# Causal attention on one NeuronCore: the high and low halves of the values held side by side as one 128-column weight

## The chip, the cores and the metric

The kernel runs on one core of a Trainium2 chip. The metric is the device time of one execution in microseconds (us); lower is better. Products run on TensorE (PE, with its weight loads shown apart as PEld), element-wise work on VectorE (DVE), ScalarE (ACT) and GpSimd (POOL). Products write to PSUM, an accumulator memory of eight banks with 512 float32 columns each; everything else lies in SBUF.

## The reference

A decoder trunk of two layers over 1024 positions with 1024 features. The first layer mixes latent attention (8 heads, keys of 96, values of 64) and a short gated convolution, the second is a state-space mixer, and each is followed by a gated feed-forward part with a short convolution. Only the attention matters here:

```python
def causal_block_attention(q, k, v):
    for i in range(seq // Q_BLOCK):          # 8 blocks of 128 queries
        lo, hi = i * Q_BLOCK, (i + 1) * Q_BLOCK
        s = jnp.einsum("bqhd,bkhd->bhqk", q[:, lo:hi], k[:, :hi]).astype(jnp.float32) * scale
        s = jnp.where(causal, s, -jnp.inf)
        p = jax.nn.softmax(s, axis=-1).astype(v.dtype)
        outs.append(jnp.einsum("bhqk,bkhd->bqhd", p, v[:, :hi]))
```

Everything is float32. The kernel keeps that precision by splitting an operand into a high part, rounded to the type float32r, and a low part, the rest. A product of two such operands is made from three: high by high, high by low, low by high (`PASSES` in the code).

## The kernel before

Attention is one stage of the kernel, between the input projection and the first feed-forward part. Its order is written out by hand; the instructions of an engine run in the order of the code. Eight steps (`Step`) cover four groups (`gr`) of two heads and two halves (`hf`) of the 1024 positions. A step has eight items (`Item`): four blocks of 128 queries (`i`) by two heads (`h`). The block number is `qb` = 4 hf + i, and the item takes in `qb` + 1 blocks of 128 keys. Over all items that makes 8 heads x 36 = 288 blocks of keys.

For one item, in turn:

- `scores` (TensorE): three products per 512 keys into a PSUM tile `pss`, weights `qh` or `ql` of 128 columns, moving `kh` or `kl`; then the mask as a product of `tri` and `eye`.
- `exponent`: VectorE takes the maximum of a row (`nm`), ScalarE the exponential (`pr`) and its sum. `invert` and `normalize` (VectorE) divide by that sum.
- `turn` (TensorE): the probabilities are transposed, 128 by 128, into `ptp`. ScalarE copies out the high part (`ph`, or `pair` for the second head), VectorE the low part (`lows`).
- `values` (TensorE, line 634): per block of keys three products into `po`, with the values as weight, 64 columns each: `vh` with the high probabilities, `vh` with the low, `vl` with the high.

The loop over items is pipelined: while the scores of item j are made, item j - 2 is transposed and item j - 3 meets its values. Between them stand parts of later steps: query and key products, their norms, their transposes (ScalarE makes `qh` and `kh`, VectorE `ql` and `kl`), and rows of the output projection (`row_down`), which VectorE adds to `xT`.

A PSUM tile `po` of one bank takes four items: two heads, 256 columns apart, by two blocks of queries. After the fourth, `finish_pair` copies it into the tile `a32` on ScalarE, one copy per head, rounds that to `ath` on ScalarE, and GpSimd subtracts to get `atl`. There are sixteen such finished pairs. In the order on VectorE, `finish_pair` lies behind the low parts and the sums of the item (`lows`, `others`) and ahead of the reciprocal (`invert`) and the next row addition and maximum:

```python
it.exponent()
...
others.get(j, nothing)()
finish = retire(queue.pop(0)) if len(queue) > 3 else nothing
finish()
it.invert()
```

Of the kernel before, what the change touches and what calls it, by code (L numbers as in the profile page):

```python
# [14 lines left out]
AF = mybir.ActivationFunctionType  # L15
ALU = mybir.AluOpType
# [4 lines left out]
P = 128  # L21
# [9 lines left out]
VD = 64  # L31
# [19 lines left out]
def hybrid_trunk_kernel(ctx: ExitStack, tc: tile.TileContext, xt, gains, mix_w_in, w_uq, w_ukv, q_gain, k_gain,  # L51
                        mix_w_out, ssm_w_in, lambda_re, lambda_im, log_step, b_re, b_im, c_re, c_im, d_skip, w_glu,
                        ffn_w_up, ffn_w_down, rope_cos, rope_sin, causal, eye16, halves, out, dbg=None):
    nc = tc.nc
# [112 lines left out]
    PASSES = ((0, 0), (0, 1), (1, 0))  # L167
# [103 lines left out]
    for gr in range(2):  # L271
        gts = []
        for i in range(2):
# [6 lines left out]
            t = pB.tile([P, S + 2], F32, tag="ut", name="ut")  # L280
# [27 lines left out]
    with phase("pc") as pC, tc.tile_pool(name="psa", bufs=1, space=PSUM, reuse_waits="tile") as pa:  # L308
# [38 lines left out]
        for tabs, row in ((tabq, qrow), (tabk, krow)):  # L347
            for j, (tab, g0) in enumerate(((cos_t, NOPE), (sin_t, NOPE + 16), (cos_t, NOPE + 16), (sin_t, NOPE))):
                nc.gpsimd.tensor_tensor(out=tabs[j], in0=tab,
                                        in1=row[:, g0:g0 + 16].unsqueeze(1).broadcast_to([P, NB, 16]),  # L350
                                        op=ALU.mult)
# [79 lines left out]
        class Step:  # L431
# [20 lines left out]
            def kv_products(self, c, bank=ps_p):  # L452
                gr, hf = self.gr, self.hf
                if c == 0:
                    self.kn = qtile("kn")
                    vt = (atile if gr % 2 else lambda name: vtile(name, F32R))("vt")
                    vv = vt.rearrange("p (t i h n) -> p t i h n", t=2, i=4, h=2)
                    self.vh, self.vl = vv[:, 0], vv[:, 1]
                ps = bank("pkv")
                for i in range(2):  # L460
                    b = 4 * hf + 2 * c + i
                    for k in range(2):
                        for ci, wi in PASSES:
                            nc.tensor.matmul(ps[:, 256 * i:256 * i + 256], lhsT=ckT[k][ci][:, P * b:P * b + P],
                                             rhs=wkv[k][wi][:, 256 * gr:256 * gr + 256],
                                             start=(k == 0 and ci == 0 and wi == 0), stop=(k == 1 and ci == 1))
                pf = ps.rearrange("p (a n) -> p a n", n=P)
                kf = self.kn.rearrange("p i h n -> p (i h) n")
                vhf = self.vh.rearrange("p i h n -> p (i h) n")[:, 4 * c:4 * c + 4, :]
                vlf = self.vl.rearrange("p i h n -> p (i h) n")[:, 4 * c:4 * c + 4, :]  # L470
                nc.scalar.activation(vhf, pf[:, :, NOPE:P], AF.Copy)
                nc.scalar.activation(kf[:, 4 * c:4 * c + 4, 0:NOPE], pf[:, :, 0:NOPE], AF.Copy)
                nc.vector.tensor_tensor(out=vlf, in0=pf[:, :, NOPE:P], in1=vhf.bitcast(F32), op=ALU.subtract)
# [77 lines left out]
        both = lambda f, *args: [f(c, *args) for c in range(2)]  # L551
# [6 lines left out]
        for n in range(8):  # L558
            if n == 4:
                wkv = [split_w(w, nc.vector) for w in wkv_raw]  # L560
            kind, p = ("kv", "q")[n // 4], n % 4
# [10 lines left out]
        class Item:  # L572
# [57 lines left out]
            def values(self, po, c0):  # L630
                for kb in range(self.qb + 1):
                    sk = self.steps[kb // 4]
                    for vi, pi in PASSES:
                        nc.tensor.matmul(po[0:VD, c0:c0 + P], lhsT=(sk.vh, sk.vl)[vi][:, kb % 4, self.h, :],  # L634
                                         rhs=self.pt[kb // 4][pi][:, P * (kb % 4):P * (kb % 4) + P],
                                         start=(kb == 0 and vi == 0 and pi == 0), stop=(kb == self.qb and vi == 1))

        def row_down(k, f):

# [12 lines left out]
        def finish_pair(grp, po, hf, i2):  # L652
            a32 = small([P, 256], "a32", "a32", 1)
            for h in range(2):
                nc.scalar.activation(a32[VD * h:VD * h + VD, :], po[0:VD, 256 * h:256 * h + 256], AF.Copy)
            cols = slice(HALF * hf + 256 * i2, HALF * hf + 256 * i2 + 256)
            nc.scalar.activation(grp.at[0][:, cols], a32, AF.Copy)
            nc.gpsimd.tensor_tensor(out=grp.at[1][:, cols], in0=a32, in1=grp.at[0][:, cols].bitcast(F32),
                                    op=ALU.subtract)
# [5 lines left out]
        def retire(item):  # L665
            st, i, h = item.st, item.i, item.h
            if i % 2 == 0 and h == 0:
                st.po = ps_t("po")
            item.values(st.po, 256 * h + P * (i % 2))
            if i % 2 == 0 or h == 0:  # L670
                return lambda: None

            def finish():
                if st.hf == 0 and i == 1:
                    groups[st.gr] = Group(st.gr)
                finish_pair(groups[st.gr], st.po, st.hf, i // 2)
                if st.hf == 1 and i == 3 and st.gr < 2:
                    rows_left.extend((st.gr, f) for f in range(KT))

            return finish  # L680
# [1084 lines left out]
    for m in range(FIRST, NM):  # L1765
        p = pairs[m]
# [106 lines left out]
```

## Time and profile before

| | |
|---|---|
| Time, median of 3 runs (lowest to highest) | 2345.22 us (2342.04 to 2348.31) |
| The profiled execution's own time | 2344.66 us |
| Its span, first to last instruction | 2342.9 us |
| Instructions | 29810 |
| PE busy over the span | 2248.5 us, 96% |
| DVE busy | 1614.7 us, 69% |
| ACT busy | 851.3 us, 36% |
| POOL busy | 767.0 us, 33% |
| Stretch of the scores and values | about 275 to 512 us |

The profile is one execution of the program, taken by the hardware. A busy share is an average over stages with different limits, and TensorE's products are pipelined: a product's record of 220 ns overlaps those before and behind it, so what counts is the distance from one to the next. The time of a change is read from the stage in which it lies and from the chain of work that ended last there.

### The profile page before, as it was taken

The page shows a single profiled execution, that of the slowest core. Times are in us where ns is not written, and L with a number is a line of the kernel's source. Part 1 is how long each engine was busy: PE and PEld are TensorE (multiplying, and loading weights), DVE is VectorE, ACT ScalarE, POOL GpSimd, SP SyncE. Part 2 cuts the span into 40 slices and gives each one's busy share as a digit, 9 for nine tenths or more (in the row PEclk, how much of TensorE's full clock was granted, in tenths as well). Part 3 has the DMA queues.
Part 4 walks back from the last instruction along what each step waited for, and adds up shares of the span by engine and source line. Part 5 has one row for each costly group of instructions (what it writes and reads, how often), then busy time and mean ns, then how long its engine had stood idle before and what let it go on. Part 6 is the DMA issues. An engine that isn't in the chain of part 4 may idle for free.

```text
span 2342.9 us, 29810 instructions
## 1 busy us (share of the span) xinstructions
PE 2248.5 (96%) x11228; PEld 1867.9 (80%) x11228; DVE 1614.7 (69%) x2650; ACT 851.3 (36%) x1446; POOL 767.0 (33%) x575
## 2 busy tenths in 40 slices
PE   7999899999999999999999988999789999999999
PEld 6888888888788878888888877788568888878887
DVE  6344677787978778879777487323888888876542
ACT  4112566664232333332223255312444444443110
POOL 4322454435233222232224344431043333324220
PEclk9999999999999999999999998999999999999999
DMA  4112000012122221223332288521132222245301
GB/s 155 45 38 57 1 10 10 10 46 72 29 66 62 82 68 49 76 80 92 101 102 63 93 223 242 171 72 41 54 110 93 82 81 81 81 153 181 125 10 72
DMA packets 227152, 192.04 MB, mean 82 GB/s; under 512 B 25472, under 2 KB 202944, under 8 KB 227008
## 3 DMA queue, kind: packets, MB, share of 16 engines
q1 hardware_dynamic: 227008, 190.14, 26.9%
q8 instruction: 88, 1.44, 0.2%
q14 instruction: 56, 0.46, 0.1%
HBM read 148.22 MB, written 46.07 MB: 83 GB/s over the span
## 4 chain that ended last, share of the span: by engine, by line
PE 79%; DVE 11%; issue 3%; DMA 3%; ACT 3%; POOL 1%; SPq 0%; DVEq 0%; POOLq 0%; ACTq 0%
PE pu L175 31%; PE pd L190 22%; PE pc L1648 4%; PE pb L1648 4%; PE pa L1648 4%; PE pd L1648 2%; PE pu L1554 1%; PE pss L586 1%; PE po L634 1%; PE pckv L378 1%; PE pq L446 1%; PE ptp L615 1%; DVE xT L1696 1%; PE pcq L378 1%; PE pda L644 1%
## 5 line engine op out<-in xcount | busy, mean ns | idle before, releaser
L154 POOL TENSOR_TENSOR wl<-raw,wh 128x1024 fp32r<-128x1024 f32 (+2 forms) x115 | 289.1, 2515 | 487.3 <-ACT wh L153 242.3
L193 DVE TENSOR_TENSOR xT<-pd,xT 128x512 f32<-128x512 f32 x320 | 204.3, 682 | 160.4 <-PE pd L190 159.8
L153 ACT ACTIVATE wh<-raw 128x1024 fp32r<-128x1024 f32 (+2 forms) x117 | 122.4, 1051 | 305.8 <-PE pu L175 212.6
L175 PE MATMUL pu<-f_h,wh 128*128 128x512 f32 x704 | 219.4, 393 | 0.0
L175 PE MATMUL pu<-f_l,wh 128*128 128x512 f32 x704 | 217.2, 390 | 0.0
L175 PE MATMUL pu<-f_h,wl 128*128 128x512 f32 x704 | 216.7, 389 | 0.0
L175 PEld LDWEIGHTS pu<-f_l,wh 128*128 128x128 f32 x704 | 132.1, 188 | 27.9
L175 PEld LDWEIGHTS pu<-f_h,wl 128*128 128x128 f32 x704 | 132.1, 188 | 27.9
L175 PEld LDWEIGHTS pu<-f_h,wh 128*128 128x128 f32 x704 | 130.7, 188 | 28.7 <-issue 1.7
L810 POOL TENSOR_TENSOR gl<-c,gh 128x512 fp32r<-128x512 f32 x44 | 61.4, 1415 | 247.0 <-ACT gh L809 247.0
L1696 DVE SCALAR_TENSOR_TENSOR xT<-u,vec,xT 128x1024 f32<-128x1024 f32 x84 | 111.1, 1330 | 13.3 <-ACT xT L1694 12.6
L759 DVE TENSOR_TENSOR u<-pu,f_rb 128x512 f32<-128x512 f32 x88 | 56.8, 685 | 89.9 <-PE pu L175 87.9
L190 PE MATMUL pd<-gh,wh 128*128 128x512 f32 x352 | 113.5, 403 | 5.4 <-DVE u L759 2.9
L190 PE MATMUL pd<-gh,dwh 128*128 128x512 f32 x352 | 108.8, 390 | 2.5 <-DVE xT L193 1.5
L190 PE MATMUL pd<-gl,wh 128*128 128x512 f32 x352 | 110.4, 395 | 0.0
L190 PE MATMUL pd<-gh,wl 128*128 128x512 f32 x352 | 110.0, 394 | 0.0
L190 PE MATMUL pd<-gh,dwl 128*128 128x512 f32 x352 | 108.5, 389 | 0.0
L190 PE MATMUL pd<-gl,dwh 128*128 128x512 f32 x352 | 108.4, 389 | 0.0
L1796 POOL TENSOR_TENSOR dwl<-raw,dwh 128x1024 fp32r<-128x1024 f32 x20 | 60.8, 3066 | 112.5 <-PE pd L190 84.3
L761 ACT ACTIVATE c<-u,vec 128x512 f32<-128x512 f32 x88 | 59.9, 717 | 69.5 <-DVE u L759 69.1
L190 PEld LDWEIGHTS pd<-gh,wh 128*128 128x128 f32 x352 | 65.8, 191 | 22.6 <-DVE xT L193 4.0
L190 PEld LDWEIGHTS pd<-gh,dwh 128*128 128x128 f32 x352 | 66.1, 188 | 16.9 <-DVE xT L193 1.9
(569 smaller groups left out, 5790.6 us busy)
## 6 DMA issues: line engine op xcount, KB each, us to landing
raw<-in_ffn_w_up_dram SPq DMA_DIRECT2D x50, 512.0 KB, 3.8
raw<-in_ffn_w_down_dram SPq DMA_DIRECT2D x42, 512.0 KB, 4.4
xT<-in_ffn_w_up_dram SPq DMA_DIRECT2D x40, 512.0 KB, 3.6
gfd<-xT SPq DMA_DIRECT2D x21, 512.0 KB, 2.6
raw<-gfd SPq DMA_DIRECT2D x20, 512.0 KB, 4.0
raw<-in_w_glu_dram SPq DMA_DIRECT2D x16, 512.0 KB, 4.0
raw<-in_mix_w_in_dram SPq DMA_DIRECT2D x14, 512.0 KB, 3.9
xT<-in_xt_dram SPq DMA_DIRECT2D x8, 512.0 KB, 7.6
```

The lines of the kernel that those rows point to most:

```text
L153: nc.scalar.activation(h[:, 0:n], raw[:, 0:n], AF.Copy)
L154: eng.tensor_tensor(out=l[:, 0:n], in0=raw[:, 0:n], in1=h[:, 0:n].bitcast(F32), op=ALU.subtract)
L175: nc.tensor.matmul(ps[hf], lhsT=w[wi][:, P * k:P * k + P], rhs=xs[k][xi][:, HALVES[hf]], start=(k == 0 and wi == 0 and xi == 0), stop=(k = ...
L190: nc.tensor.matmul(ps[hf], lhsT=ws[i][wi][:, P * f:P * f + P], rhs=gts[i][xi][:, HALVES[hf]], start=(i == first and wi == 0 and xi == 0), ...
L193: nc.vector.tensor_tensor(out=xT[f][:, HALVES[hf]], in0=ps[hf], in1=xT[f][:, HALVES[hf]], op=ALU.add)
L378: nc.tensor.matmul(ps[:, HALF * j:HALF * j + n], lhsT=xa[k][xi][:, P * (2 * p + j):P * (2 * p + j) + P], rhs=w[k // kw][wi][:, n * (k % kw ...
L759: nc.vector.tensor_tensor(out=u[:, 2:HALF + 2], in0=ps[hf], in1=rb[:, HALVES[hf]], op=ALU.mult)
L761: nc.scalar.activation(c, u[:, 2:HALF + 2], AF.Copy, scale=cwcol(layer, 2, m))
L810: nc.gpsimd.tensor_tensor(out=gl[:, cols], in0=cv[hf], in1=gh[:, cols].bitcast(F32), op=ALU.subtract)
L1648: nc.tensor.matmul(ps, lhsT=w[:, HALF * wi + P * k:HALF * wi + P * k + P], rhs=x.at(xi, k), start=(start and k == 0 and wi == 0 and xi == ...
L1696: nc.vector.scalar_tensor_tensor(out=c, in0=u[:, w:S + w], scalar=cwcol(self.layer, w, m), in1=c, op0=ALU.mult, op1=ALU.add)
L1796: eng.tensor_tensor(out=l, in0=raw, in1=h.bitcast(F32), op=ALU.subtract)
```

## The change

The tile of the values, 1024 columns, is laid out anew. Before, all high parts stood ahead of all low parts. Now the high and the low part of one block and head stand side by side, 64 + 64 columns, so that they make one weight of 128 columns. Each block of keys then has two products: this weight with the high probabilities, and with the low ones. The upper 64 rows of the result hold what the high values give, the lower 64 rows what the low values give (the product of low by low comes with it). The two halves are added in `finish_pair`: ScalarE copies the lower half from PSUM, VectorE adds the upper half to it.

```diff
@@ kv_products
-                    vv = vt.rearrange("p (t i h n) -> p t i h n", t=2, i=4, h=2)
-                    self.vh, self.vl = vv[:, 0], vv[:, 1]
+                    vv = vt.rearrange("p (i h t n) -> p i h t n", t=2, i=4, h=2)
+                    self.vh, self.vl = vv[:, :, :, 0], vv[:, :, :, 1]
+                    self.v = vt.rearrange("p (i h n) -> p i h n", i=4, h=2)
@@ values
-                    for vi, pi in PASSES:
-                        nc.tensor.matmul(po[0:VD, c0:c0 + P], lhsT=(sk.vh, sk.vl)[vi][:, kb % 4, self.h, :],
+
+                    for pi in range(2):
+                        nc.tensor.matmul(po[:, c0:c0 + P], lhsT=sk.v[:, kb % 4, self.h, :],
                                          rhs=self.pt[kb // 4][pi][:, P * (kb % 4):P * (kb % 4) + P],
-                                         start=(kb == 0 and vi == 0 and pi == 0), stop=(kb == self.qb and vi == 1))
+                                         start=(kb == 0 and pi == 0), stop=(kb == self.qb and pi == 1))
@@ finish_pair
             for h in range(2):
-                nc.scalar.activation(a32[VD * h:VD * h + VD, :], po[0:VD, 256 * h:256 * h + 256], AF.Copy)
+                rows, both = slice(VD * h, VD * h + VD), slice(256 * h, 256 * h + 256)
+                nc.scalar.activation(a32[rows, :], po[VD:P, both], AF.Copy)
+                nc.vector.tensor_tensor(out=a32[rows, :], in0=po[0:VD, both], in1=a32[rows, :], op=ALU.add)
```

The order of instructions differs at two places that matter. The first is on TensorE, in the last item of the second group's second half (`qb` = 7, eight blocks of keys). A shape there is rows of the result by moving columns. Before:

```order
L532 MATMUL ptqk<-ident,kn 96x128 [waits Pool_49]
L532 MATMUL ptqk<-ident,kn 96x128 x3
L634 MATMUL po<-pair,vt 64x128 x24
L586 MATMUL pss<-kh,qh 128x256 [waits PE_49,Activation_49]
L586 MATMUL pss<-kl,qh 128x256
L586 MATMUL pss<-kh,ql 128x256
```

and with the change:

```order
L533 MATMUL ptqk<-ident,kn 96x128 [waits Pool_49]
L533 MATMUL ptqk<-ident,kn 96x128 x3
L636 MATMUL po<-pair,vt 128x128 x16
L587 MATMUL pss<-kh,qh 128x256 [waits PE_49,Activation_49]
L587 MATMUL pss<-kl,qh 128x256
L587 MATMUL pss<-kh,ql 128x256
```

Twenty-four products have become sixteen, with 128 result rows each in place of 64; what stands around them is the same.

The second is the finished pair of that half's first two blocks, on VectorE. In brackets stand the engines whose semaphore an instruction waits for. Before, VectorE has no part in it:

```order
L627 TENSOR_TENSOR pl<-ptp,ph 128x512 [waits Activation_49]
L627 TENSOR_TENSOR pl<-ptp,ph 128x384 [waits Activation_49]
L535 SCALAR_TENSOR_TENSOR ql<-ptqk,gq,qh 96x512 [waits Activation_49]
L505 TENSOR_REDUCE kv<-sqk 128x4 [waits Activation_49]
L603 RECIPROCAL rs<-sm 128x1
L646 TENSOR_TENSOR xT_90<-pda,xT_90 128x1024
L595 TENSOR_REDUCE nm<-pss 128x1 [waits PE_49]
```

With the change, two additions (`a<-po,a`) stand between the sums `kv` and the reciprocal `rs`:

```order
L628 TENSOR_TENSOR pl<-ptp,ph 128x512 [waits Activation_49]
L628 TENSOR_TENSOR pl<-ptp,ph 128x384 [waits Activation_49]
L536 SCALAR_TENSOR_TENSOR ql<-ptqk,gq,qh 96x512 [waits Activation_49]
L506 TENSOR_REDUCE kv<-sqk 128x4 [waits Activation_49]
L659 TENSOR_TENSOR a_3674<-po,a_3674 64x256 [waits Activation_49,Pool_49]
L659 TENSOR_TENSOR a_3674<-po,a_3674 64x256 [waits Activation_49]
L604 RECIPROCAL rs<-sm 128x1
L648 TENSOR_TENSOR xT_90<-pda,xT_90 128x1024
L596 TENSOR_REDUCE nm<-pss 128x1 [waits PE_49]
```

On ScalarE the same pair was two copies in a row and the rounding copy:

```order
L504 ACTIVATE sqk<-kn 128x4x64 [waits Activation_49]
L655 ACTIVATE a_3776<-po 64x256 [waits PE_49]
L655 ACTIVATE a_3776<-po 64x256
L657 ACTIVATE ath_3271<-a_3776 128x256 [waits Activation_49]
L622 ACTIVATE pair<-ptp 128x512 [waits PE_49,Pool_49]
L622 ACTIVATE pair<-ptp 128x384 [waits PE_49]
```

and is now

```order
L505 ACTIVATE sqk<-kn 128x4x64 [waits Activation_49]
L658 ACTIVATE a_3674<-po 64x256 [waits PE_49]
L658 ACTIVATE a_3674<-po 64x256 [waits DVE_49]
L661 ACTIVATE ath_3201<-a_3674 128x256 [waits DVE_49]
L623 ACTIVATE pair<-ptp 128x512 [waits PE_49]
L623 ACTIVATE pair<-ptp 128x384 [waits PE_49,Pool_49]
```

The second copy and the rounding copy now each wait for VectorE, and each of VectorE's additions waits for ScalarE. The line numbers behind line 455 move by one to four with the change.

## Rows read from the trace of the kernel before

**Rows 1.** First line of the page: the span of the profiled execution.
```profile
span 2342.9 us, 29810 instructions
```

**Rows 2.** Two stretches: length, busy us of PE, PEld, DVE, ACT, POOL, granted clock.
```profile
275.00:512.00 237.00, 220.63 (x1939) 201.60 (x1939) 187.77 (x364) 147.74 (x353) 101.88 (x170) 0.99 0.06 17
450.00:480.00 30.00, 25.74 (x218) 23.23 (x219) 21.14 (x47) 15.92 (x42) 11.16 (x20) 0.94 0.00 1
```

**Rows 3.** Chain that ended last, 255 to 530 us: first and last of 24 `po` pieces.
```profile
286.52 0.56 PE po L634 x9
492.16 1.08 PE po L634 x18
```

**Rows 4.** Same chain at first and last of eleven finished pairs.
```profile
298.06 0.75 DVE kl L535
299.33 0.87 DVE nm L595
...
475.82 0.75 DVE ql L535
476.64 0.59 DVE nm L595
```

**Rows 5.** Line 634, the products with the values: count, duration min/median/max.
```profile
L634 PE MATMUL po<-pair,vt x432: 218/223/358, 278.0 to 511.5; 128*64 128x128 f32 x144
L634 PE MATMUL po<-ph,vt x288: 220/223/455, 273.9 to 508.6; 128*64 128x128 f32 x144
L634 PE MATMUL po<-pl,vt x144: 221/223/308, 274.0 to 508.5; 128*64 128x128 f32 x144
```

**Rows 6.** TensorE in order of time, products with the values (start, us).
```profile
293.33 0.23 PE L634 MATMUL po<-pl,vt 128*64 128x128 f32 x1
293.39 0.28 PE L634 MATMUL po<-ph,vt 128*64 128x128 f32 x2
293.51 0.22 PE L634 MATMUL po<-pl,vt 128*64 128x128 f32 x1
```

**Rows 7.** TensorE, scores with 128-column weights and 128 moving columns.
```profile
287.66 0.22 PE L586 MATMUL pss<-kh,qh 96*128 96x128 f32 x1
287.72 0.27 PE L586 MATMUL pss<-kl,qh 96*128 96x128 f32 x1
287.83 0.28 PE L586 MATMUL pss<-kh,ql 96*128 96x128 f32 x1
287.94 0.28 PE L590 MATMUL pss<-tri,eye 128*128 128x128 f32 x1
```

**Rows 8.** ScalarE around the finished pair of 378 us.
```profile
378.10 0.77 ACT L655 ACTIVATE a<-po 64x256 f32<-64x256 f32 x2
378.90 0.42 ACT L657 ACTIVATE ath<-a 128x256 fp32r<-128x256 f32 x1
381.37 1.11 ACT L598 ACTIVATE pr<-pss,nm 128x1024 f32<-128x1024 f32 x1 [0.74 <-DVE nm L595]
```

**Rows 9.** VectorE around the same pair.
```profile
377.94 0.75 DVE L535 SCALAR_TENSOR_TENSOR ql<-ptqk,gq,qh 96x512 fp32r<-96x512 f32 x1 [0.88 <-ACT qh L534]
378.61 0.41 DVE L505 TENSOR_REDUCE kv<-sqk 128x4 f32<-128x256 f32 x1
378.94 0.15 DVE L603 RECIPROCAL rs<-sm 128x1 f32<-128x1 f32 x1
380.13 1.21 DVE L595 TENSOR_REDUCE nm<-pss 128x1 f32<-128x1024 f32 x1
```

**Rows 10.** Groups of line and shape, 262 to 514 us: count, busy, mean ns.
```profile
L473 DVE TENSOR_TENSOR vt<-pkv,vt 128x256 fp32r<-128x256 f32 x12 | 5.1, 423 | 6.5 <-ACT kn L472 6.5
L472 ACT ACTIVATE kn<-pkv 128x256 f32<-128x256 f32 x12 | 4.6, 386 | 0.0
```

**Rows 11.** End of the stage, all engines in order of time.
```profile
511.77 0.77 ACT L655 ACTIVATE a<-po 64x256 f32<-64x256 f32 x2 [5.12 <-PE po L634]
513.04 0.50 PE L190 MATMUL pd<-ath,wh 128*128 128x512 f32 x1 [0.75 <-ACT ath L657]
```

## The prediction

> **What bounds the kernel now.** First the span: the profiled execution has 2342.9 us from first to last instruction [rows 1] and 2344.66 us as a run, against a median of 2345.22 for the three timed runs; my sum is made against 2344.66, which lies 0.6 below that median. A measurement of this kernel tells 0.3% (7.0 us) from no change, hardly less.
>
> Then the stage. All that is changed runs in the attention stage, so I read the busy times of that stretch, 275 to 512 us, not of the whole span. In its 237 us TensorE is busy 220.6, VectorE 187.8, ScalarE 147.7 [rows 2]. TensorE leads, VectorE stands at 79%, and neither is a bound by itself: each waits for the other at times.
>
> Then the chain that ended last, through this stage. It passes through the products with the values (`po`, line 634) in 24 pieces, from 9 products at 286.5 us to 18 at 492.2 us; the counts of the 24 add up to 366 products [rows 3] of the 864 that the line issues (432 + 288 + 144) [rows 5]. That is 122 of 288 blocks of keys, at three products each. Elsewhere it stands on VectorE. In particular, at eleven of the sixteen finished pairs it enters VectorE by the low part of a key or query (`kl`, `ql`), and goes on there, with no wait for another engine, to the row additions and the next maximum (`nm`). The first is at 298 to 299 us, the last at 476 us [rows 4]. The new additions are put between exactly these two instructions.
>
> **The products.** 288 are removed (one of three per block), 576 remain, and these have weights of 128 columns in place of 64. The price of one is what matters. Before, the start of one `pl` product to the next, with two `ph` products between them, is 293.51 - 293.33 = 0.18 us for three: 60 ns each [rows 6].
>
> No product with the values has a 128-column weight yet. The nearest rows are the scores of a diagonal block: the same float32r type, weights of 128 columns, 128 moving columns. Their records start unevenly, so I read ends (start plus duration): 287.88, 287.99, 288.11, 288.22. Three steps in 0.34 us: 113 ns each [rows 7]. The first two have the same weight (`qh`) and still stand 0.11 apart, so a second product with one weight isn't cheaper. With the 512 moving columns or with 128, each product brings its own load; at 128 the load of 128 columns sets the pace.
>
> So a block costs 2 x 113 = 226 ns, where it cost 3 x 60 = 180: 46 ns more, not 60 less. From both sides: 60 ns each would make it 120, 113 makes it 226. I take 113, since type, weight and moving columns are all the same as in the changed product; the old rows differ from it in the very thing that is changed. On the chain: 122 x 46 ns = **5.6 us**. All 288 blocks: 13.2 us.
>
> The Trainium skill, in "TensorE: Matmul & The Clock Gate" (Weight-path perf modes — Fast Weight Load (FWL) and DoubleRow), says that weights are loaded faster when there are 128 of them and the type isn't FP32, which a 64-column weight doesn't get. By that rule the change would have the load hidden and 60 ns per product. The rows of the scores, with 128 weights of float32r at 113 ns, speak against it here; I keep it as a rival.
>
> **The finished pairs.** There are sixteen. ScalarE's two copies (0.77 us together, 0.385 each) were followed at once by its rounding copy of 0.42 us at 378.90 [rows 8]. VectorE had nothing in this. Now it has two additions of 64x256. No such row is there; the nearest is a VectorE operation with one operand from PSUM, one from SBUF and 256 elements per partition, 423 ns [rows 10]. Fewer partitions can hardly cost more, and nothing cheaper of 256 elements shows; I take 0.41.
>
> The order of the change has ScalarE's second copy wait for VectorE, and VectorE's second addition for that copy. So from the first addition on it goes in turn: addition 0.41, copy 0.385, addition 0.41, with a handover between two engines of 0.03 (the maximum ends at 380.13 + 1.21 = 381.34 [rows 9], the exponential starts at 381.37 [rows 8]). That is 0.41 + 0.03 + 0.385 + 0.03 + 0.41 = 1.265, which I round to 1.25 us of VectorE's time. The first copy is hidden: at this pair it ends at 378.10 + 0.385 = 378.49, while VectorE is busy up to about 378.94 with the sums for the keys [rows 9]. If that cover were gone, 0.45 more.
>
> Behind the additions on VectorE's queue stand the reciprocal, the row addition and the next item's maximum; ScalarE's exponential waits for that maximum, and two items later TensorE's transposes wait for the normalised row. In the old order VectorE goes from the sums at 378.61 to the reciprocal at 378.94 without a pause [rows 9], so nothing swallows the 1.25 there. Bounds for one pair: nothing, if VectorE would have waited that long anyway, and 1.25 + 0.45. On ScalarE the rounding copy and the copies queued behind it (`pair`, `ph`) go back by about as much; they are wanted one item later, after the delayed maximum, so I count nothing for them. Eleven pairs on the chain: 11 x 1.25 = **13.8 us**.
>
> The last pair stands alone: after it TensorE waits 0.75 us for the rounding copy before the output projection starts [rows 11]. There two additions and their handovers lie bare, 2 x 0.41 + 3 x 0.03 = **0.9 us**.
>
> **What I count as nothing.** The values are written in strides (128x4x64 in place of 128x256), with as many elements and instructions. A ScalarE write into a strided tile (`kn`, 64 of 96 columns) takes 386 ns per 256 elements [rows 10], where the compact copies of 256 elements take 385 [rows 8], so strides cost nothing there. On VectorE no strided row of that kind is at hand; doubling its sixteen would be 16 x 0.42 = 6.7 us, an unlikely bound. Transfers, GpSimd and the order outside this stage stay as they were.
>
> **The sum.** 5.6 + 13.8 + 0.9 = 20.3 us. A chain whose links keep their order grows by all that is put into it, so this is nearer a floor. Off the chain stay 166 blocks x 46 ns = 7.6 us and four pairs x 1.25 = 5.0 us, 12.6 together. They lie where another engine ended last; part of that cover is used up by now, and I take a fifth, 2.5. Forecast: 2344.7 + 20.3 + 2.5 = 2367.5, say **2367 us**, +0.9%. Its own range is 2359 to 2374.
>
> **The rivals.**
> 1. *Both costs add up.* TensorE's 13.2 and VectorE's 15 x 1.25 = 18.8, with the last 0.9, all come onto the path, since the two engines take turns in it: +32.9, 2377.6. Longer waits of TensorE could also bring more stretches of half clock: 450 to 480 us has a granted clock of 0.94 [rows 2], that is 30 x 0.06 x 2 = 3.6 us at 1.2 GHz in place of 2.4, some 1.8 us lost. Two more: 2381. For it: both engines are close to full. Against it: a delay on one gives the other time to catch up.
> 2. *VectorE has room.* It is idle for 237 - 187.8 = 49 us of the stage. If that took in the additions: 5.6 + 0.9 = +6.5, 2351, within 0.3%. Against it: at eleven pairs the old chain runs through VectorE without a pause.
> 3. *The weight load is hidden behind the product before it*, as a 64-column one was, at 60 ns per product. The place is line 634, the price is 180 - 120 = 60 ns less per block, and it decides from 90 ns per product down. Where TensorE alone sets the stage, this gives 288 x 60 ns = 17.3 us less: 2327, faster. With the additions on the chain as I count them, it is 13.8 + 0.9 - 122 x 60 ns = +7.4: 2352. Against it: 113 ns in the scores.
> 4. *The change doesn't do what it says.* The order shows it done, sixteen products where there were 24, so I give this nothing.
>
> **How the numbers follow.** Forecast 0.66, both costs added 0.20, VectorE with room 0.07, hidden loads 0.07, of which 0.03 with TensorE alone as the bound. Faster: 0.03. Same: 0.07 and most of the other 0.04, 0.10. Slower: 0.87. The range leaves out the rivals at 2352 and below (0.14) and little else: 2355 to 2383.
>
> **What the profile of the changed kernel would show.** `po` products with weights of 128 columns, ending 110 to 115 ns apart (60 would prove rival 3). Line 634's successor with 576 products, taking 576 x 113 = 65 us where 864 x 60 = 52 were. At each pair a VectorE addition of about 0.41, a ScalarE copy, an addition, and the reciprocal 1.2 to 1.3 later than before. The stretch from the first scores to the output projection some 23 us longer, everything behind it as long as before. Wrong would make it: additions of 0.2 or 0.8 us, VectorE standing idle before the additions because the copy comes late, or a stage that grows by much less than the old chain's 20.

## The result, and the profile after

The change made the kernel slower: 2378.61 us median of four runs (2374.26 to 2383.25) against 2345.87 (2342.04 to 2348.31). The ratio is 1.0141, with a 95% interval of 1.0116 to 1.0166: 33 us, between 27 and 39. The profiled execution took 2374.26 us. It is the lowest of the four, so the profile shows some 30 of the 33 us. The forecast was 2367 us, with a range of 2355 to 2383.

The head of the page, to set against [rows 1]:

```profile
span 2372.5 us, 29294 instructions
...
PE 2265.5 (95%) x10940; PEld 1881.8 (79%) x10940; DVE 1623.6 (68%) x2682; ACT 854.0 (36%) x1446; POOL 763.5 (32%) x575
```

TensorE has 288 products fewer and is busy 17 us longer; VectorE has 32 instructions more and is busy 9 us longer. The whole difference lies in the attention stage. From the start of the first mask product (line 590, now 591) to the start of the last product of the output projection in that stage (`pd<-ath`, `pd<-atl`) it was 264.0 to 530.5 us, 266.6 us; now it is 262.3 to 559.4, 297.1 us. That is 30.5 longer; the whole span grew by 29.6. I call this the stage length from here on.

The products, line 636 of the changed kernel, by count and duration, against [rows 5]:

```profile
L636 PE MATMUL po<-pair,vt x288: 218/275/455, 275.4 to 536.2; 128*128 128x128 f32 x144
...
L636 PE MATMUL po<-ph,vt x144: 221/275/456, 271.3 to 532.9; 128*128 128x128 f32 x144
...
L636 PE MATMUL po<-pl,vt x144: 272/275/415, 271.4 to 533.0; 128*128 128x128 f32 x144
...
its engine sat idle before it (us, times) until:
  DVE a L659: 10.8, 13
```

576 in place of 864, as said. The last line is new: before thirteen of them TensorE sat idle until an addition of VectorE (`a`, line 659) had ended. And one after the other, against [rows 6]:

```profile
387.43 0.28 PE L636 MATMUL po<-pl,vt 128*128 128x128 f32 x1
387.54 0.28 PE L636 MATMUL po<-ph,vt 128*128 128x128 f32 x1
387.65 0.28 PE L636 MATMUL po<-pl,vt 128*128 128x128 f32 x1
387.76 0.28 PE L636 MATMUL po<-ph,vt 128*128 128x128 f32 x1
387.87 0.28 PE L636 MATMUL po<-pl,vt 128*128 128x128 f32 x1
```

They start 110 ns apart, also the two of a block, which share a weight, where the old ones stood at 60 ns. The finished pair that [rows 8, 9] showed, on ScalarE and VectorE:

```profile
384.86 0.38 ACT L658 ACTIVATE a<-po 64x256 f32<-64x256 f32 x1 [0.30 <-PE po L636]
...
384.95 0.40 DVE L506 TENSOR_REDUCE kv<-sqk 128x4 f32<-128x256 f32 x1
...
385.34 0.42 DVE L659 TENSOR_TENSOR a<-po,a 64x256 f32<-64x256 f32 x1
...
385.79 0.38 ACT L658 ACTIVATE a<-po 64x256 f32<-64x256 f32 x1 [0.55 <-DVE a L659]
...
386.20 0.42 DVE L659 TENSOR_TENSOR a<-po,a 64x256 f32<-64x256 f32 x1 [0.44 <-ACT a L658]
386.65 0.17 DVE L604 RECIPROCAL rs<-sm 128x1 f32<-128x1 f32 x1
386.65 0.42 ACT L661 ACTIVATE ath<-a 128x256 fp32r<-128x256 f32 x1 [0.48 <-DVE a L659]
...
387.85 1.22 DVE L596 TENSOR_REDUCE nm<-pss 128x1 f32<-128x1024 f32 x1
```

Addition, copy, addition in turn, each waiting for the other engine (the brackets), and the reciprocal 1.3 us behind the sums `kv`, which end at 385.35. From the start of the first addition to the end of the second it is 1.27 or 1.28 us at all sixteen pairs. And at all sixteen the chain that ended last now passes through both additions and the copy between them (start and length in us):

```profile
385.34 0.43 DVE a L659
...
385.79 0.39 ACT a L658
...
386.20 0.42 DVE a L659
```

The stretch of the stage by engine, against [rows 2]:

```profile
275.00:540.00 265.00, 238.44 (x1643) 217.28 (x1642) 196.05 (x391) 150.88 (x353) 100.13 (x171) 0.96 0.05 15
```

The columns behind the length are the busy times of TensorE's matmuls and weight loads, VectorE, ScalarE and GpSimd, and the granted clock, 0.96 over 265 us where it was 0.99 over 237. By the trace's clock records TensorE stood at 1.2 GHz for 27.3 us in this stage, and at 2.4 GHz otherwise; before it was 6.8.

### The profile page after: what moved, and what is told of

Same layout as the page of the kernel before. It is cut to its first block, busy times and chain, and to the rows that moved or that the text cites. A ratio compares the mean times of both kernels' runs of the same rounds, so it can differ in the third digit from the quotient of the medians.

```text
span 2372.5 us, 29294 instructions
## 1 busy us (share of the span) xinstructions
PE 2265.5 (95%) x10940; PEld 1881.8 (79%) x10940; DVE 1623.6 (68%) x2682; ACT 854.0 (36%) x1446; POOL 763.5 (32%) x575
## 4 chain that ended last, share of the span: by engine, by line
PE 79%; DVE 11%; issue 3%; ACT 3%; DMA 2%; POOL 2%; SPq 0%; DVEq 0%; ACTq 0%; POOLq 0%
PE pu L175 30%; PE pd L190 22%; PE pc L1652 4%; PE pb L1652 4%; PE pa L1652 4%; PE pd L1652 2%; PE po L636 2%; PE pu L1558 1%; PE pss L587 1%; PE pda L646 1%; PE pckv L378 1%; PE ptp L616 1%; PE pq L446 1%; DVE xT L1700 1%; PE pcq L378 1%
## 5 line engine op out<-in xcount | busy, mean ns | idle before, releaser
L1700 DVE SCALAR_TENSOR_TENSOR xT<-u,vec,xT 128x1024 f32<-128x1024 f32 x84 | 111.1, 1329 | 13.3 <-ACT xT L1698 12.6
```

What stands on the lines that cost most here:

```text
L1700: nc.vector.scalar_tensor_tensor(out=c, in0=u[:, w:S + w], scalar=cwcol(self.layer, w, m), in1=c, op0=ALU.mult, op1=ALU.add)
```

## The experiments

All times are medians, and each run is compared with runs of the kernel before on the same chip, whose medians were 2345.35 to 2345.78. The first four divide the change into its products and its finished pairs.

**e1_products**, the products alone. ScalarE copies the upper half, the lower is left out:

```diff
 (after)
-                nc.scalar.activation(a32[rows, :], po[VD:P, both], AF.Copy)
-                nc.vector.tensor_tensor(out=a32[rows, :], in0=po[0:VD, both], in1=a32[rows, :], op=ALU.add)
+                nc.scalar.activation(a32[VD * h:VD * h + VD, :], po[0:VD, 256 * h:256 * h + 256], AF.Copy)
```

> The change's products alone: weights of 128 columns, two products per block, but the finished pair as before (ScalarE copies the upper half only; the lower half is left out of the result). Theory A, both parts cost and add up (products some 7 to 10 us net, the finished pairs some 20 to 23): 2352 to 2357 us. Rival B, the products cost nearly all, by 13 us of TensorE's time and by stretches of half clock, and the additions are hidden: 2368 to 2380. Rival C, the finished pairs cost nearly all: 2345 to 2350. In all three the products end 112 ns apart and TensorE does not wait for VectorE at the first product of a pair.

Measured: 2351.59 us, ratio 1.0026 (1.0017 to 1.0036), 6.0 us more. The stage is 6.2 us longer in the profiled execution (2357.68 us; 6.8 of its 13.0 us of longer span lie outside the stage, where nothing was changed). That lies between theories A (2352 to 2357) and C (2345 to 2350), and far from B: the dearer products are a small part of the loss.

**e2_finish**, the finished pairs alone: before, with the change's copy and addition, both of the upper half.

```diff
 (before)
-                nc.scalar.activation(a32[VD * h:VD * h + VD, :], po[0:VD, 256 * h:256 * h + 256], AF.Copy)
+                rows, both = slice(VD * h, VD * h + VD), slice(256 * h, 256 * h + 256)
+                nc.scalar.activation(a32[rows, :], po[0:VD, both], AF.Copy)
+                nc.vector.tensor_tensor(out=a32[rows, :], in0=po[0:VD, both], in1=a32[rows, :], op=ALU.add)
```

> The change's finished pair alone: three products of 64 columns as before, but each head's copy is followed by VectorE's addition of the same upper half (so the result of attention is doubled), with the same waits as in the change. Theory A: TensorE waits at the first product of the next pair for the second addition, 13 to 15 times by 0.5 to 1.3 us, and VectorE's chain grows by 1.25 us per pair: 2363 to 2369 us. Rival B (hidden additions): within 0.3% of before, below 2352. Rival C (the finished pairs alone make the change's 30 us): 2372 or more.

Measured: 2367.57 us, ratio 1.0090 (1.0075 to 1.0105), 22.0 us more; stage 20.3 longer. Theory A. As in the change, the chain that ended last passes through the additions of all sixteen pairs. TensorE stood at 1.2 GHz for 10.2 us of the stage, where it was 6.8 before; those 3.4 us cost at most half of that, so the clock hardly has a part in the 20.3. The waits of this run, longest first in total (who waited for whom: us in total, times, longest):

```profile
ACT a L656 <- DVE a L657: 14.5, 16, 2.1
...
PE po L634 <- DVE a L657: 12.4, 14, 1.2
...
ACT ath L659 <- DVE a L657: 7.7, 16, 0.5
```

TensorE's wait stands here with the old products, so it belongs to the finish.

**e3_gpsimd**, the change with the halves added by GpSimd:

```diff
 (after)
+            b32 = small([P, 256], "b32", "b32", 1)
             for h in range(2):
                 rows, both = slice(VD * h, VD * h + VD), slice(256 * h, 256 * h + 256)
-                nc.scalar.activation(a32[rows, :], po[VD:P, both], AF.Copy)
-                nc.vector.tensor_tensor(out=a32[rows, :], in0=po[0:VD, both], in1=a32[rows, :], op=ALU.add)
+                nc.scalar.activation(b32[rows, :], po[VD:P, both], AF.Copy)
+                nc.scalar.activation(a32[rows, :], po[0:VD, both], AF.Copy)
+            nc.gpsimd.tensor_tensor(out=a32, in0=a32, in1=b32, op=ALU.add)
```

> The change with another finish: ScalarE copies all four halves out of PSUM (two copies more, 0.77 us per pair), GpSimd adds them, VectorE has no part. PSUM is then freed by ScalarE, as before. Theory A: TensorE's wait for the additions is gone, VectorE's chain is as before, what stays is the products and some of ScalarE's longer time: 2353 to 2362 us. Rival B: as the change, 2372 to 2383. Rival C with ScalarE's longer occupation as the cost of the finish: 2370 or more.

Measured: 2393.31 us, ratio 1.0202 (1.0187 to 1.0217), 47.8 us more: a miss, worse than the change itself. The waits of this run show where it went:

```profile
ACT ath L663 <- POOL a L661: 31.5, 16, 3.8
...
DVE pair L628 <- ACT pair L623: 27.3, 18, 2.8
```

ScalarE stands 31.5 us at the rounding copy: GpSimd's sixteen additions take 13.3 us of that, and the rest goes by until GpSimd has come to them. What is behind it on ScalarE stands with it: VectorE's low parts (`pair`) wait 27.3 us for ScalarE's copies of the transposed rows, where it was 3.0 before the change. Of the three only rival C, 2370 or more by ScalarE's longer turn, holds. The prediction had counted nothing for ScalarE's queue; here these waits stand in it. How much of the 47.8 us they make, and how much the 32 more copies on ScalarE (12.2 us), isn't separated.

**e4_apart**, the two lower halves copied first, side by side, to a tile of their own:

```diff
 (after)
...
+                nc.scalar.activation(b32[rows, :], po[VD:P, both], AF.Copy)
+            for h in range(2):
...
+                nc.vector.tensor_tensor(out=a32[rows, :], in0=po[0:VD, both], in1=b32[rows, :], op=ALU.add)
```

> The change with the two lower halves copied to a tile of their own, one after the other, before VectorE's two additions: ScalarE's second copy no longer waits for VectorE, both additions stand side by side (0.82 in place of 1.25 us on VectorE), and PSUM is freed some 0.4 us earlier. Theory A: about a third of the finish's cost goes, 16 x 0.42 us = 6.7 us at most: 2369 to 2375 us. Rival B: no difference from the change, 2374 to 2383.

Measured: 2374.06 us, ratio 1.0120 (1.0104 to 1.0135), 28.5 us more, some 4 less than the change; the intervals overlap. The finished pair takes 0.85 us on VectorE, where it took 1.27. In the direction of theory A, but too near to the change to count as more.

The next four take the finish apart, and ask what sets the pace of a product.

**e5_wide**, one product per block, with 256 moving columns. The high and the low probabilities lie in one tile, `both`; of that only the view that the product reads is shown:

```diff
 (e1_products)
+                    self.both = getattr(self, "both", []) + [pair.rearrange("p (t n) -> p t n", t=2)]
...
-                    for pi in range(2):
-                        nc.tensor.matmul(po[:, c0:c0 + P], lhsT=sk.v[:, kb % 4, self.h, :],
-                                         rhs=self.pt[kb // 4][pi][:, P * (kb % 4):P * (kb % 4) + P],
+                    nc.tensor.matmul(po[:, 256 * self.h:256 * self.h + 256], lhsT=sk.v[:, kb % 4, self.h, :],
+                                     rhs=self.both[kb // 4][:, :, P * (kb % 4):P * (kb % 4) + P],
...
```

> One product per block instead of two: the 128-column weight with the high and the low probabilities side by side as 256 moving columns, into 256 columns of the accumulator; the finished pair is copied as before the change. Left out of the result: the lower halves, the low probabilities' columns and one of the two query blocks of a pair. It asks what sets the pace of a product. If a product costs the longer of its load (107 to 113 ns for 128 columns) and its stream of moving columns, 256 moving columns cost 113 to 117 ns each, a block costs 115 in place of 180 before and 226 in the change, and the run ends 6 to 12 us below before: 2333 to 2340 us. Rival (the load is added to the stream, or a strided moving operand is slower): 160 ns or more each, 2345 us or more.

Measured: 2338.51 us, ratio 0.9975 (0.9965 to 0.9984), 7.3 us less than before. Its products, in order of time:

```profile
303.03 0.76 PE L635 MATMUL po<-pair,vt 128*128 128x256 f32 x5
...
306.99 0.86 PE L635 MATMUL po<-both,vt 128*128 128x256 f32 x6
```

A sixth product adds 0.10 us; the median distance over the stage is 118 ns. So a product of 256 moving columns costs nearly what one of 128 does (112), with the same weight of 128 columns, while 128 moving columns with a weight of 64 cost 60. That fits a pace set by the longer of load and stream, and not by their sum. The rival is out.

**e6_touch**, the held bank alone:

```diff
 (before, behind the two copies)
+            held = small([P, 2], "held", "held", 1)
+            nc.vector.tensor_copy(out=held[0:VD, :], in_=po[0:VD, 255:257])
```

> The kernel before with one small addition: behind ScalarE's copies VectorE reads two columns of the finished pair's accumulator. VectorE's work is nearly nothing (some 0.1 us per pair), but the PSUM bank is now freed at VectorE's place in its queue, and TensorE's first product of the next pair has to wait for that. Theory (the held bank is a cost of its own): TensorE waits there 10 or more times, 3 to 8 us in all, 2349 to 2355 us. Rival (the wait of TensorE in the change was only a sign of VectorE's longer chain, not a cost): within 2 us of before, 2344 to 2348.

Measured: 2349.41 us, ratio 1.0015 (1.0005 to 1.0025), 3.6 us more; stage 2.6 longer. Sixteen copies of 142 ns make 2.3 us of VectorE's time; TensorE's waits for them are short, as the profile of this line shows (last line: who waited for it, us in total, times):

```profile
L657 DVE COPY held<-po x16: 138/142/151, 286.4 to 514.5; 64x2 f32<-64x2 f32 x16
...
  PEld po L634: 1.9, 7
```

The theory's lower end: a bank that VectorE frees at its place in the queue is a small cost here, where VectorE's own part is short.

**e7_nopsum**, the additions without the bank:

```diff
 (e2_finish)
-                nc.vector.tensor_tensor(out=a32[rows, :], in0=po[0:VD, both], in1=a32[rows, :], op=ALU.add)
+                nc.vector.tensor_tensor(out=a32[rows, :], in0=a32[rows, :], in1=a32[rows, :], op=ALU.add)
```

> The counterpart: products as before, VectorE has its two additions of 64x256 per pair, but on the copied tile (the result of attention is doubled), so the PSUM bank is freed by ScalarE and its two copies follow each other as before. VectorE's chain grows by some 0.6 to 0.9 us per pair, TensorE doesn't wait for the additions. Theory (chain and held bank add up): 8 to 13 us over before, 2353 to 2359 us. Rival (VectorE's additions alone make the 22 us of the finished pair): 2365 or more. Rival (they are hidden, the bank does it): 2349 or less.

Measured: 2365.37 us, ratio 1.0086 (1.0070 to 1.0101), 19.6 us more: my theory missed, and the first rival holds, just. The stage grows by 20.4 us; 17.1 us more of it than before stand at 1.2 GHz (23.9 against 6.8), so up to 8.5 of the 20.4 can be the clock's. The additions have 14.7 us of work in all. The two take 0.86 us at fifteen pairs, and 2.23 at one (the last section has the reason). Their line, with count, busy time and mean in ns, and VectorE's idle time before them:

```profile
L657 DVE TENSOR_TENSOR a<-a 64x256 f32<-64x256 f32 x32 | 14.7, 458 | 4.2 <-ACT a L656 3.7
```

TensorE's wait for VectorE at the bank is gone, and has moved: to the transposes, which wait for VectorE's low parts of an earlier item (`ptp`), and to the scores, which wait for its row addition (`pss`). The first two lines are of the kernel before, the others of this run:

```profile
PE ptp L615 <- DVE pair L627: 5.2, 7, 1.9
...
PE pss L586 <- DVE xT L646: 2.0, 4, 0.5
...
PE ptp L615 <- DVE pair L627: 12.8, 16, 1.7
...
PE pss L586 <- DVE xT L646: 6.9, 8, 1.4
```

That is 12.5 us more at these two places, as much as the 12.4 at the bank in e2_finish. VectorE comes later with all that it does, and TensorE meets that at one place or another.

**e8_sbufadd**, e3_gpsimd with the addition on VectorE (`nc.vector` for `nc.gpsimd` in its last line):

> The change with another finish: ScalarE copies all four halves out of PSUM (0.77 us more per pair), and VectorE adds them in one operation of 128x256 with both operands in SBUF. The bank is freed by ScalarE. Theory: TensorE's wait for VectorE is gone, VectorE has about half the work, ScalarE waits for VectorE before its rounding copy; products 6 us, the rest 6 to 12: 2357 to 2364 us. Rival (ScalarE's longer turn costs as much as it did with GpSimd's addition): 2375 or more.

Measured: 2381.17 us, ratio 1.0151 (1.0136 to 1.0167), 35.4 us more: the rival, and another miss. One addition of 0.43 us has replaced two, and still the run is as slow as the change. The waits say how:

```profile
DVE a L661 <- ACT a L660: 19.4, 15, 5.3
...
ACT ath L663 <- DVE a L661: 9.2, 16, 0.8
```

With four copies ahead of it on ScalarE, the addition makes VectorE wait 19.4 us, and then ScalarE waits 9.2 for VectorE. VectorE has less work and is stopped for longer.

The last four separate VectorE's additions from ScalarE's wait for them.

**e9_late_add**, e7_nopsum with the rounding copy and GpSimd's subtraction one item later:

```diff
 (e7_nopsum)
+            def split():
+                nc.scalar.activation(grp.at[0][:, cols], a32, AF.Copy)
...
+            splits.append(split)
...
                         queue[-3].lows()
+                    split_pair()
```

> Products as before, VectorE's two additions per pair on the copied tile (attention doubled), but ScalarE's rounding copy and GpSimd's subtraction are issued one item later, behind that item's exponential, so ScalarE no longer waits for VectorE. Theory 1 (VectorE's chain alone makes it, 14 us of additions on its queue): 2361 to 2367 us, as with the rounding copy in its old place (2365). Theory 2 (ScalarE's queue, held at the rounding copy, makes half or more): 2350 to 2357.

Measured: 2362.49 us, ratio 1.0076 (1.0060 to 1.0093), 17.1 us more. Theory 1. It is 2.9 us less than e7_nopsum, which the intervals don't tell apart.

**e10_hold**, ScalarE's wait with little work behind it (one copy per pair in the end, behind both of ScalarE's):

```diff
 (before, behind the two copies)
+            nc.vector.tensor_copy(out=a32[:, 0:2], in_=a32[:, 0:2])
```

> The other half of it: the kernel before, where VectorE copies two columns of the finished tile onto themselves behind each of ScalarE's copies (some 0.1 us each), so that ScalarE's rounding copy waits until VectorE gets there, with hardly any work on VectorE and the PSUM bank freed by ScalarE. Theory 1: within 4 us of before, 2345 to 2350. Theory 2: 2353 to 2360.

Measured: 2354.65 us, ratio 1.0036 (1.0022 to 1.0050), 9.3 us more; stage 8.0 longer. Theory 2. VectorE has sixteen copies of mostly 0.17 us, 3.8 us in all, and ScalarE waits 8.0 us for them; e6_touch, with 2.3 us of such copies and no wait of ScalarE, cost 3.6 us:

```profile
ACT ath L658 <- DVE a L656: 8.0, 16, 1.4
```

**e11_late_apart**, e4_apart with the rounding copy one item later (the same edit as in e9_late_add):

> The change with both lower halves copied first (as in the run with the two tiles, 2374 us) and the rounding copy one item later: ScalarE waits for VectorE nowhere in a finished pair; the products, VectorE's additions and the held bank stay. Theory 1: 2370 to 2375. Theory 2: 2360 to 2367.

Measured: 2377.68 us, ratio 1.0134 (1.0119 to 1.0150), 32.3 us more, as far as the change. That is above the range of theory 1 (2370 to 2375), and farther from theory 2. ScalarE's waits at the rounding copy are down to 1.3 us, from 17.0 in e4_apart, and nothing is won. This profiled execution has a granted clock of 0.95 from 275 to 540 us.

**e12_late_before**, the control: before with that same edit.

> The control: the kernel before with nothing but the rounding copy and GpSimd's subtraction one item later. It waits for no other engine in either place, so both theories say within 3 us of before, 2343 to 2348; ScalarE's copies of the transposed rows come 0.42 us earlier at sixteen pairs, which could give back up to 3 us.

Measured: 2346.30 us, ratio 1.0007 (0.9997 to 1.0016): no difference, as both theories said.

No experiment that computes all of attention is faster than the kernel before; e5_wide, which is, leaves most of the sums out.

## Why the prediction was right, and where it was off

**The direction and the products.** Right. The price of 113 ns, read from the scores [rows 7], was measured at 110 to 113, and the term of 5.6 us on the chain at 6.0 (e1_products). The 24 pieces of the chain behind that term are those among the longest that the view lists; the whole chain has 26, with 381 products, which makes 5.8. Rival 3 fell in both its forms: with weights of 128 columns the load isn't hidden. The reading of the Trainium skill that stood beside it, "TensorE: Matmul & The Clock Gate" (Weight-path perf modes — Fast Weight Load (FWL) and DoubleRow), by which 128 weights of a type other than FP32 load faster, isn't borne out either: in float32r no faster load shows at 110 ns. What did hide the load is a longer stream (e5_wide).

**The finished pair.** Right in its make-up: 1.25 us forecast, 1.27 measured, one after the other as the order had it. Off in its count: "Eleven pairs on the chain: 11 x 1.25 = 13.8 us" and, with the last pair, 14.7. The finish alone cost 22.0 (e2_finish).
- The count came from the old chain. The new one, of the change and of the finish alone, passes through all sixteen pairs. Fifteen at 1.27 are 19.1 us, and with the 2.4 of the last pair (below) 21.5 of the 22.0. What is added can make its own path: e7_nopsum has no wait at the bank, and its chain still passes through fifteen pairs.
- "I count nothing" for ScalarE's queue was wrong by itself: a rounding copy that waits for VectorE costs 9.3 us with hardly any work on VectorE (e10_hold, its sixteen small copies included). But it doesn't show on top of the additions: taking it away gave 2.9 us, within the noise (e9_late_add), and nothing in e11_late_apart.
- I had not seen that VectorE now frees the PSUM bank of `po`, so that TensorE's first product of the next pair waits for the second addition, 13 times, 10.8 us. By itself the held bank cost 3.6 us, of which VectorE's copies may be part (e6_touch). Of the finish's 22.0 it can be 22.0 - 19.6 = 2.4, within the noise, and e7_nopsum had more of the lower clock than e2_finish.

**The last pair.** Forecast 0.9 us. TensorE's pause before the output projection was 0.75 us [rows 11]; it is now 3.19:

```profile
537.80 0.42 DVE L659 TENSOR_TENSOR a<-po,a 64x256 f32<-64x256 f32 x1 [0.44 <-ACT a L658]
...
538.25 1.23 DVE L648 TENSOR_TENSOR xT<-pda,xT 128x1024 f32<-128x1024 f32 x1
538.25 0.42 ACT L661 ACTIVATE ath<-a 128x256 fp32r<-128x256 f32 x1 [0.48 <-DVE a L659]
...
539.62 1.19 PE L190 MATMUL pd<-ath,wh 128*128 128x512 f32 x2 [3.19 <-DVE u L759]
```

That is 2.4 us more. The rounding copy ends at 538.67, but the output projection starts at 539.62: it waits for VectorE's row addition (line 648, 1.23 us) and a small clearing (`u`) behind it. That row addition now stands behind the two additions; before, it ran at 510.27, ahead of this pair's copies. The prediction had not seen this.

**The sum.** The measured 2378.6 lies outside the forecast's own range of 2359 to 2374, and inside the stated one only because that took in the rival *Both costs add up*. The parts make 6.0 + 22.0 = 28.0, within the interval of the change's 33. The forecast's 22.8 gave the off-chain work a fifth, which was right for the products and far too little for the pairs. The rival's 32.9 came nearer, but in part by luck: it had 13.2 for the products, where e1_products showed 6.0, and 19.7 for the finish, where e2_finish showed 22.0. The other 5 us aren't told from the noise. One candidate is the clock: 10.2 us of the stage at 1.2 GHz in either part alone, 27.3 in the change. The 17.1 us between them cost TensorE at most half of that, 8.5. The rival had named it with 2; no run here changed the clock by itself, and waits that lower it can't be told from a clock that makes waits, so it is open.

**VectorE has room** was plainly wrong. The finish alone cost 22.0 us, more than the 13.2 of VectorE's additions, so the 49 us in which VectorE is idle took in none of them. In the stretch of the changed kernel it is idle for 265 - 196 = 69 us: these are waits for ScalarE and TensorE, and they grow with the chain.

## What to carry to other kernels

Here a product cost the longer of its weight load and its moving stream: 60 ns with 64 weight and 128 moving columns, 112 with 128 and 128, 118 with 128 and 256. A wider weight paid only where the moving side was widened with it. Before work is moved from TensorE to a finish that two engines share, count the handovers: VectorE, idle a fifth of this stage, had no room for work that its partners wait for. The old chain gives a floor for what is added. In this stage, where the engines take turns, it had eleven of the sixteen pairs, and the new one all of them: what is added can make its own path, so count it at the other places too.

## What the runs showed of the hardware that was not expected

In the change ScalarE's second copy only reads `po`, and stood waiting for a VectorE addition that only reads it too. With the additions on the copied tile (e7_nopsum), or with both copies ahead of the additions (e4_apart), the second copy waits for no addition. So in this program two engines that only read one PSUM tile run in the order of the code, as they would around a write.

VectorE's additions of 64x256 took 0.42 us with an operand in PSUM and as much from SBUF alone, but one of the latter took 1.77. It met GpSimd's long subtraction `wl`, and ended 0.28 us behind it. The first two lines are of e7_nopsum (the second is both additions of the pair), the third of the change:

```profile
380.40 2.39 POOL L154 TENSOR_TENSOR wl<-raw,wh 128x1024 fp32r<-128x1024 f32 x1 [8.68 <-PE po L634]
...
381.30 2.23 DVE L657 TENSOR_TENSOR a<-a 64x256 f32<-64x256 f32 x2
...
384.51 2.39 POOL L154 TENSOR_TENSOR wl<-raw,wh 128x1024 fp32r<-128x1024 f32 x1 [9.79 <-PE po L636]
```

The same befell an addition of e9_late_add (1.07 us), the one of e8_sbufadd (0.67 in place of 0.43) and the small copy of e10_hold (1.29 in place of 0.17), each with all its operands in SBUF, and each ended 0.02 to 0.28 us behind that subtraction. In the change both additions of 385.34 and 386.20, with an operand in PSUM, lay within it and took 0.42 us as always.

The spread of the runs goes with the granted clock. Of e1_products' ten runs the five with a granted clock of 0.986 or 0.987 took 2348.84 to 2350.08 us, the two at 0.982 took 2357.18 and 2357.68: a difference of 0.004 to 0.005 in the mean clock stands beside some 8 us. One of the latter is its profiled execution, so its profile is read here by its stage and not by its span.
